# Row sums of 64 MB on one core: the scaling of the last results moved to GpSimd, and the last store cut in two halves of 64 partitions on two queues

## Chip, cores, metric

One core of one Trainium2 chip. The time is the device's, in microseconds, median of several executions. Every execution quoted was in the fast state, at a granted clock of 1.0, or, where there was a single look (e14, e15, e17), at a clock of 1.0 and of unknown state.

Words used below: the issue of a DMA is the instruction that starts it, its landing the last of the semaphore increments that report it done. The DRAIN of an engine stands in its closing part, ahead of its report to the barrier; the closing barriers are where all engines wait for each other at the end of the program. DVE is VectorE, ACT is ScalarE, POOL is GpSimd, SP is SyncE. A line such as `L193` is a line of that kernel's program; the same statement has other line numbers in other kernels. "Columns" are fp32 values of one partition.

## The reference

```python
x: float32 [32, 512, 1024]
def reference(x, divisor):                 # divisor = 1024.0
    return (np.sum(x, axis=-1) / divisor).astype(np.float32)
```

16,384 rows of 1024 values, so 128 per partition. 112 per partition go through large tiles (result `res`, stored early), the last 16 through ever smaller ones (result `fin`).

## The kernel before

The parts that matter, with cuts marked. `landed` is a semaphore of its own for the last store: the program's closing barriers run while that store is under way, and SyncE waits for it last.

```python
def close_while_storing(nc, landed):
    ...                                    # cut: finds the last store, takes it out of the body
    end.instructions = [
        with_sync(drain, on_wait=tuple(needs.values())),      # SyncE: wait for all other work
        with_sync(store, on_wait=(done,), on_update=(add,)),  # the store waits for VectorE alone
        *end.instructions[1:-1],                              # the barriers of all engines
        with_sync(last, on_update=(sub,)),                    # wait for landed >= 16
    ]
...
    res = one.tile([P, M], F32, name="res")
    fin = one.tile([P, L], F32, name="fin")
    q = one.tile([P, L], F32, name="q")
    r = one.tile([P, L], F32, name="r")    # L = 16
    nc.gpsimd.memset(r, 0.0)
...                                        # cut: loads and sums of all rows but the last two
    c = 768
    row = one.tile([P, D], F32, name="row")
    load(row, x_last[:, j, :])
    act_sum(r[:, j : j + 1], row[:, c:], by=scale)
    nc.vector.reduce_sum(out=q[:, j : j + 1], in_=row[:, :c], axis=AX)

    a, b = 448, 704                        # the very last row comes in three pieces
    pa = one.tile([P, a], F32, name="pa")
    pb = one.tile([P, b - a], F32, name="pb")
    pc = one.tile([P, D - b + 2], F32, name="pc")
    load(pa, x_last[:, L - 1, :a])
    load(pb, x_last[:, L - 1, a:b])
    load(pc[:, : D - b], x_last[:, L - 1, b:])
    nc.gpsimd.tensor_scalar_mul(out=res, in0=res, scalar1=scale)
    tc.keep_in_program_order(nc.sync.dma_start(out=o_main, in_=res))

    act_sum(pc[:, D - b : D - b + 1], pa)
    nc.vector.reduce_sum(out=pc[:, D - b + 1 :], in_=pb, axis=AX)
    nc.vector.scalar_tensor_tensor(
        out=fin[:, : L - 1], in0=q[:, : L - 1], scalar=scale, in1=r[:, : L - 1], op0=MULT, op1=ADD
    )
    scaled = one.tile([P, D - b + 2], F32, name="scaled")
    nc.vector.tensor_scalar(
        out=scaled, in0=pc, scalar1=scale, scalar2=0.0, op0=MULT, op1=ADD, accum_out=fin[:, L - 1 :]
    )
    tc.keep_in_program_order(nc.sync.dma_start(out=o_last, in_=fin))
```

## Time and profile before

| | before |
|---|---|
| time, median of the first 3 runs | 161.4 us (161.34 to 161.51) |
| span of the profile | 159.8 us |
| DMA queue, share of the span | 98.0% |
| last VectorE result | 158.28 us |
| issue of the last store, its landing | 158.31 us, 159.73 us |

The span is the time from the first to the last instruction in the profile; the time of that execution was 161.31 us, so 1.55 us lie outside the span. The DMA queue is full nearly all the way, so the change was aimed at the last 2 to 3 us, behind the last bytes. The lines of the profile stand in the prediction.

### The profile page before, as it was taken

The page shows a single profiled execution, that of the slowest core. Times are in us where ns is not written, and L with a number is a line of the kernel's source. Part 1 is how long each engine was busy: PE and PEld are TensorE (multiplying, and loading weights), DVE is VectorE, ACT ScalarE, POOL GpSimd, SP SyncE. Part 2 cuts the span into 40 slices and gives each one's busy share as a digit, 9 for nine tenths or more (in the row PEclk, how much of TensorE's full clock was granted, in tenths as well). Part 3 has the DMA queues.
Part 4 walks back from the last instruction along what each step waited for, and adds up shares of the span by engine and source line. Part 5 has one row for each costly group of instructions (what it writes and reads, how often), then busy time and mean ns, then how long its engine had stood idle before and what let it go on. Part 6 is the DMA issues. An engine that isn't in the chain of part 4 may idle for free.

```text
span 159.8 us, 139 instructions
## 1 busy us (share of the span) xinstructions
DVE 121.1 (76%) x17; ACT 19.6 (12%) x37; POOL 0.8 (0%) x6
## 2 busy tenths in 40 slices
DVE  0500059995999599978999599959995996494985
ACT  3000000000000000000000000000001900480973
POOL 0000000000000000000000000000000000001000
DMA  7999999978999999978999999978999999899993
GB/s 250 472 459 459 459 459 459 459 330 359 459 459 459 459 459 459 459 316 373 459 459 459 459 459 459 416 345 388 459 459 427 394 480 505 353 435 390 408 400 132
DMA packets 2592, 67.18 MB, mean 420 GB/s; under 512 B 544, under 2 KB 928, under 8 KB 1056
## 3 DMA queue, kind: packets, MB, share of 16 engines
q1 hardware_dynamic: 2592, 67.18, 98.0%
HBM read 67.11 MB, written 0.07 MB: 420 GB/s over the span
## 4 chain that ended last, share of the span: by engine, by line
DMA 76%; DVE 22%; SPq 1%; issue 0%; DVEq 0%
DMA t<-in_x_dram 56%; DMA row<-in_x_dram 21%; DVE res L153 20%; SPq L142 1%; DVE q L176 1%; DVE scaled L198 0%; DVE pc L193 0%; DVE fin L194 0%; DVEq L198 0%; DVEq L232 0%
## 5 line engine op out<-in xcount | busy, mean ns | idle before, releaser
L153 DVE TENSOR_REDUCE res<-t 128x14 f32<-128x14336 f32 (+3 forms) x9 | 111.2, 12360 | 34.3 <-DMA t<-in_x_dram 34.3
L147 ACT ACTIVATE junk<-t 128x1024 f32<-128x1024 f32 x16 | 16.2, 1013 | 135.9 <-DMA t<-in_x_dram 135.9
L153 DVE TENSOR_REDUCE q<-t 128x4 f32<-128x4096 f32 (+2 forms) x3 | 7.9, 2642 | 2.7 <-DMA t<-in_x_dram 2.5
L147 ACT ACTIVATION_READ_ACCUMULATOR junk<-t 128x1 f32 x16 | 3.0, 187 | 0.0
L147 ACT ACT_TABLE_LOAD x1 | 1.3, 1283 | 1.7 <-PEq L218 1.7
L189 POOL TENSOR_SCALAR res<-res 128x112 f32<-128x112 f32 x1 | 0.5, 494 | 143.8 <-DVE res L153 143.8
L176 DVE TENSOR_REDUCE q<-row 128x1 f32<-128x768 f32 x1 | 1.0, 953 | 0.0
L198 DVE TENSOR_SCALAR_CACHE_REDUCE scaled<-pc 128x322 f32<-128x322 f32 x1 | 0.5, 490 | 0.1
L147 ACT ACTIVATE junk<-pa 128x448 f32<-128x448 f32 x1 | 0.5, 548 | 0.0
L193 DVE TENSOR_REDUCE pc<-pb 128x1 f32<-128x256 f32 x1 | 0.4, 414 | 0.0
L147 ACT ACTIVATE junk<-row 128x256 f32<-128x256 f32 x1 | 0.4, 388 | 0.1
L194 DVE SCALAR_TENSOR_TENSOR fin<-q,r 128x15 f32<-128x15 f32 x1 | 0.2, 176 | 0.0
L147 ACT ACTIVATION_READ_ACCUMULATOR junk<-pa 128x1 f32 x1 | 0.2, 186 | 0.0
L147 ACT ACTIVATION_READ_ACCUMULATOR junk<-row 128x1 f32 x1 | 0.2, 185 | 0.0
L139 POOL MEMSET r<- 128x16 f32 x1 | 0.1, 112 | 1.3 <-POOLq L218 1.3
L218 POOL MEMSET const-bfloat16-1.0<- 128x1 bf16 x1 | 0.1, 103 | 0.0
L218 POOL MEMSET const-uint8-127<- 128x1 uint8 x1 | 0.1, 102 | 0.0
L218 POOL MEMSET const-float32-0.0<- 128x1 f32 x1 | 0.1, 99 | 0.2 <-issue 0.2
L218 POOL MEMSET const-float32-1.0<- 128x1 f32 x1 | 0.1, 99 | 0.0
L198 DVE DVE_READ_ACCUMULATOR scaled<-pc 128x1 f32 x1 | 0.1, 83 | 0.0
## 6 DMA issues: line engine op xcount, KB each, us to landing
t<-in_x_dram SPq DMA_DIRECT2D x7, 7168.0 KB, 35.7
t<-in_x_dram SPq DMA_DIRECT2D x1, 6144.0 KB, 33.3
t<-in_x_dram SPq DMA_DIRECT2D x1, 4096.0 KB, 26.1
t<-in_x_dram SPq DMA_DIRECT2D x2, 1024.0 KB, 18.6
t<-in_x_dram SPq DMA_DIRECT2D x1, 2048.0 KB, 30.5
row<-in_x_dram SPq DMA_DIRECT2D x1, 512.0 KB, 33.2
pa<-in_x_dram SPq DMA_DIRECT2D x1, 224.0 KB, 33.3
pc<-in_x_dram SPq DMA_DIRECT2D x1, 160.0 KB, 33.1
```

What stands on the lines that cost most here:

```text
L139: nc.gpsimd.memset(r, 0.0)
L142: tc.keep_in_program_order(nc.sync.dma_start(out=dst, in_=src))
L147: nc.scalar.activation(junk[:, :n], src, COPY, scale=by, accum_out=dst)
L153: nc.vector.reduce_sum(out=dst[:, :d], in_=t[:, :d, :], axis=AX)
L176: nc.vector.reduce_sum(out=q[:, j : j + 1], in_=row[:, :c], axis=AX)
L189: nc.gpsimd.tensor_scalar_mul(out=res, in0=res, scalar1=scale)
L193: nc.vector.reduce_sum(out=pc[:, D - b + 1 :], in_=pb, axis=AX)
L194: nc.vector.scalar_tensor_tensor(out=fin[:, : L - 1], in0=q[:, : L - 1], scalar=scale, in1=r[:, : L - 1], op0=MULT, op1=ADD)
L198: nc.vector.tensor_scalar(out=scaled, in0=pc, scalar1=scale, scalar2=0.0, op0=MULT, op1=ADD, accum_out=fin[:, L - 1 :])
L218: nc = _bacc.Bacc("TRN2", target_bir_lowering=False, num_devices=1)
```

## The change

The intent: free VectorE, which runs its last four operations nearly back to back, of one of them (the scaling of 15 columns goes to GpSimd) and of 64 columns of another (768 becomes 704); and cut the last store in halves that go out from two queues at once, so that it would land sooner. As `r` now holds one column, it is made one column wide. Two lines that order the semaphore waits of a DMA are cut below; all kernels of the experiments that were built from the changed kernel, and e1, e2, e11 and e13, have them too.

```diff
@@ close_while_storing @@
+    for engine in (SP, ACT):
+        half = [... last DMA copy of that engine ...][-1]
+        ...
+        halves[engine] = with_sync(half, on_update=(add,))
...
-    last = nc.sync.wait_ge(landed, 16).ins
+    last = nc.sync.wait_ge(landed, 32).ins
...
-        with_sync(store, on_wait=(done,), on_update=(add,)),
+        with_sync(halves[SP], on_wait=(done,)),
@@ the kernel @@
-    r = one.tile([P, L], F32, name="r")
-    nc.gpsimd.memset(r, 0.0)
+    r = one.tile([P, 1], F32, name="r")
...
-    c = 768
+    c = 704
...
-    act_sum(r[:, j : j + 1], row[:, c:], by=scale)
+    act_sum(r, row[:, c:], by=scale)
...
-    nc.vector.scalar_tensor_tensor(
-        out=fin[:, : L - 1], in0=q[:, : L - 1], scalar=scale, in1=r[:, : L - 1], op0=MULT, op1=ADD
+    nc.gpsimd.tensor_scalar_mul(out=fin[:, :j], in0=q[:, :j], scalar1=scale)
+    nc.gpsimd.tensor_scalar(
+        out=fin[:, j : j + 1], in0=q[:, j : j + 1], scalar1=scale, scalar2=r, op0=MULT, op1=ADD
     )
...
-    tc.keep_in_program_order(nc.sync.dma_start(out=o_last, in_=fin))
+    H = P // 2
+    tc.keep_in_program_order(nc.sync.dma_start(out=o_last[:H], in_=fin[:H]))
+    nc.scalar.dma_start(out=o_last[H:], in_=fin[H:])
```

More of the change, by code (lines that the diff above doesn't have):

```diff
@@ L15 @@
 SP = mybir.EngineType.SP
+ACT = mybir.EngineType.Activation
 def start_loads_at_once(nc):
@@ L53, in rank @@
     def rank(i, w):
+        if type(i).__name__ == "InstDMACopy":
+            return 1 if w.ant_name.startswith("DVE_") else 2
         own = {"DVE": "DVE_", "Activation": "Activation_", "SP": "DVE_", "Pool": "DVE_"}
@@ L71, in close_while_storing @@
     body, end = nc.main_func.blocks[1], nc.main_func.blocks[-1]
-    store = [i for i in body.instructions if i.engine == SP and type(i).__name__ == "InstDMACopy"][-1]
-    (lane,) = store.sync_info.on_update
     drain = end.instructions[0]
@@ L76, in close_while_storing @@
     needs = {w.id: w for w in drain.sync_info.on_wait}
-    assert needs[lane.id].wait_value > lane.update_value
-    needs[lane.id] = dataclasses.replace(
-        needs[lane.id], wait_value=needs[lane.id].wait_value - lane.update_value
-    )
-    (done,) = [w for w in store.sync_info.on_wait if w.ant_name.startswith("DVE_")]
+    own = dict(sync_type="semaphore", id=landed.num, ant_name=landed.name)
+    add = mybir.SyncUpdate(update_mode="sem-add-imm", update_value=16, **own)
+    sub = mybir.SyncUpdate(update_mode="sem-sub-imm", update_value=32, **own)
+    halves = {}
+    for engine in (SP, ACT):
+        half = [i for i in body.instructions if i.engine == engine and type(i).__name__ == "InstDMACopy"][-1]
+        (lane,) = half.sync_info.on_update
+        assert needs[lane.id].wait_value >= lane.update_value
+        needs[lane.id] = dataclasses.replace(
+            needs[lane.id], wait_value=needs[lane.id].wait_value - lane.update_value
+        )
+        halves[engine] = with_sync(half, on_update=(add,))
+    (done,) = [w for w in halves[SP].sync_info.on_wait if w.ant_name.startswith("DVE_")]
     assert needs[done.id].wait_value == done.wait_value
     del needs[done.id]
-    own = dict(sync_type="semaphore", id=landed.num, ant_name=landed.name)
-    add = mybir.SyncUpdate(update_mode="sem-add-imm", update_value=16, **own)
-    sub = mybir.SyncUpdate(update_mode="sem-sub-imm", update_value=16, **own)
-    last = nc.sync.wait_ge(landed, 16).ins
+    last = nc.sync.wait_ge(landed, 32).ins
     assert nc.main_func.blocks[-1].instructions[-1].name == last.name
-    body.instructions = [i for i in body.instructions if i.name != store.name]
+    body.instructions = [
+        halves[ACT] if i.name == halves[ACT].name else i
+        for i in body.instructions
+        if i.name != halves[SP].name
+    ]
     end.instructions = [
-        with_sync(drain, on_wait=tuple(needs.values())),
-        with_sync(store, on_wait=(done,), on_update=(add,)),
+        with_sync(drain, on_wait=tuple(w for w in needs.values() if w.wait_value)),
+        with_sync(halves[SP], on_wait=(done,)),
         *end.instructions[1:-1],
```

## The prediction

> **What bounds the kernel now.** I read the page first (busy tenths, rates, the chain that ended last), then the chain of work and the timeline of the last 5 us, the waits of the DMA queue, and last the DMA issues.
>
> The page's second and third parts: busy tenths in 40 slices of 4 us, and the queue's share of the span.
>
> ```profile
> DVE  0500059995999599978999599959995996494985
> DMA  7999999978999999978999999978999999899993
> q1 hardware_dynamic: 2592, 67.18, 98.0%
> HBM read 67.11 MB, written 0.07 MB: 420 GB/s over the span
> ```
>
> The 16 DMA engines are taken for 98% of the span and VectorE (DVE) for 76%: 67 MB of input at 420 GB/s set the time. The change touches no load, so about 157 of the 161 us are out of its reach. What is left is the tail, behind the last bytes. The timeline from 155 us on (start, duration):
>
> ```profile
> 156.18 0.39 ACT L147 ACTIVATE junk<-row 128x256 f32<-128x256 f32 x1
> 156.18 0.95 DVE L176 TENSOR_REDUCE q<-row 128x1 f32<-128x768 f32 x1
> 156.50 0.18 ACT L147 ACTIVATION_READ_ACCUMULATOR junk<-row 128x1 f32 x1
> 156.72 0.55 ACT L147 ACTIVATE junk<-pa 128x448 f32<-128x448 f32 x1
> 157.17 0.18 DVE L194 SCALAR_TENSOR_TENSOR fin<-q,r 128x15 f32<-128x15 f32 x1
> 157.20 0.19 ACT L147 ACTIVATION_READ_ACCUMULATOR junk<-pa 128x1 f32 x1
> 157.26 0.41 DVE L193 TENSOR_REDUCE pc<-pb 128x1 f32<-128x256 f32 x1
> 157.79 0.49 DVE L198 TENSOR_SCALAR_CACHE_REDUCE scaled<-pc 128x322 f32<-128x322 f32 x1
> 158.20 0.08 DVE L198 DVE_READ_ACCUMULATOR scaled<-pc 128x1 f32 x1
> 158.31 0.34 SPq L201 DMA_DIRECT2D out_dram<-fin  x1
> ```
>
> See that DVE runs four instructions without a pause from 156.18 to 158.28 us, and that ScalarE (ACT) is done at 157.39. The store starts 0.03 us after DVE. The DMA issues (last column: us from issue to landing), with the waits of the DMA queue:
>
> ```profile
> pc<-in_x_dram SPq DMA_DIRECT2D x1, 160.0 KB, 33.1
> pb<-in_x_dram SPq DMA_DIRECT2D x1, 128.0 KB, 33.1
> out_dram<-res SPq DMA_DIRECT2D x1, 56.0 KB, 11.5
> out_dram<-fin SPq DMA_DIRECT2D x1, 8.0 KB, 1.4
> ```
>
> ```profile
> SPq L232 <- DMA out_dram<-res: 0.6, 1, 0.6
> SPq L201 <- DVE scaled L198: 0.5, 1, 0.5
> ```
>
> Added to their issue times in the trace (123.87, 124.39, 146.17, 158.31), the records put the landings at 157.02 (pb), 157.50 (pc), 157.71 (the big store of res) and 159.73 us (the last store). The span ends at 159.76. So from 156.18 on DVE is the bound: pc has been there for 0.29 us when the last operation starts at 157.79, and SyncE has been free since 157.78 for a store that starts at 158.31. After that comes one store of 8 KB that takes 1.42 us. Its parts by the trace's records: 0.34 us issue, 0.50 us until the first packet (159.15), 0.21 us of packets (to 159.36), then the 16 semaphore increments arrive from 159.56 to 159.73, most 8 ns apart. The barriers that close the program run beside it and end at about 159.50, so they have 0.25 us to spare.
>
> **What the Trainium skill says.** "DMA: Bandwidth & Descriptors", Rules for kernel authors, has this very case: two transfers to disjoint partition halves are not worth it, for both spread over the same 16 engines; one transfer of 128 partitions is advised. Its section Issuing engines are not separate DMA queues says that issuing from several engines only saves sequencer time. The trace has only one queue so far and can't show it[...]. "Perfetto Trace Analysis", DMA Instruction — HWDGE, says that the descriptor generator is shared between sequencers and locked while one uses it; no run here shows it yet. "GPSIMD Engine Reference", 3.1, gives a GpSimd instruction two software dispatch hops; [...]494 ns for 112 columns, while a memset of 16 columns takes 112 ns.
>
> **The change part by part.**
>
> 1. The row is split 704/320 instead of 768/256. DVE reductions to one column take 1220 ns (1024 elements), 953 (768) and 414 (256), so (953-414)/512 = 1.05 ns an element: 704 elements take 886 ns, 67 ns less. ACT: (548-388)/192 = 0.83 ns an element, so 320 take 441 ns, 53 ns more. ACT's next operation waits for pa (landed 156.70, start 156.72); with the longer row ACT is ready at about 156.66. So ACT's end stays at 157.39.
>
> 2. The 15-column scaling leaves DVE. It cost 157.26-157.13 = 0.12 us between the row reduction's end and the pb reduction's start (the latter overlaps its tail). Now the row ends at 156.18+0.89 = 157.07, and pb may follow at once: pb landed at 157.02, and DVE started 0.02 us after a landing in the case of row. So pb starts at 157.04 to 157.08, ends at 157.46 to 157.50.
>
> 3. The last operation started 0.12 us after the pb reduction's end (157.79-157.67). So it starts at 157.57 to 157.62. Other floors: pc's landing 157.50+0.02; ACT's 157.39. Both hold less than 0.1 us before it, so about a further 0.05 us of speed-up would have been lost. It is 0.49 us long, so the store can be issued at 158.10 to 158.14: gain 0.17 to 0.22 us, taken as 0.20.
>
> 4. GpSimd does the scaling instead. The 14 columns need the next-to-last row's results (156.16): start 156.2, an estimate of 0.3 us from the 494 ns. The single column needs the row reduction (157.07) and takes an estimated 0.3 to 0.4 us: done by about 157.5. That is 0.5 us before DVE's last operation ends at about 158.07. So both lie beside other work, at a cost of 0. The memset of r falls away at 1.7 us, where nothing waits for it.
>
> 5. The store in halves. Each engine still gets eight 64-byte descriptors, and two completion descriptors instead of one, so the packets save nothing. 32 increments must reach one semaphore; if they come 8 ns apart as in before, that is 0.13 us more than 16. If the issue of a half is shorter than 0.34 us, some is won back: the input loads of 1 to 7 MB have issues of 0.33 to 0.47 us, as long as the 8 KB store's, so the issue hardly goes by size and I expect at most 0.05 us. If the generator is shared, the half that comes second is late by some part of 0.34 us. I take +0.10 us as the middle, from -0.05 to +0.40.
>
> Sum: -0.20 + 0.10 = -0.10 us, 161.4 to 161.3 us, with the span going from 159.8 to 159.7.
>
> **Rivals.** A: the halves run truly side by side, each with shorter issue and packets, and the store shortens by 0.1 us or more: 161.4-0.2-0.1 = 161.1. For it: most of the 1.42 us is latency, and two latencies can overlap. Against it: they overlap with nothing that was serial before, as the size of the store was hardly in the 1.42. B: the halves serialize, or ACT's first and only DMA issue is slow to start: +0.35 on the store eats the 0.20 gained, 161.55. For it: the skill's locked generator. Also, the closing barriers wait for ACT's issue too; with 0.25 us to spare they would bind only if ACT's issue took over 0.6 us. C: the gain on DVE is lost because GpSimd becomes the last producer: the two stores and the closing drain wait for it. It would need the one-column operation to take over 0.9 us, against 0.49 for 112 columns; then 161.4 or more. D: a second DMA queue costs something outside the span (time minus span is now 161.3-159.8 = 1.5 us, of which the profile shows nothing): by its nature not to be sized here.
>
> **Range and chances.** The three runs before spread 0.17 us by themselves, and loads may land differently by as much from run to run. Parts 1 to 3 are sure to about 0.05 us, part 5 is the loose one, from -0.05 to +0.40; so 160.95 to 161.65, and 161.25 as the single number, a little under the sum, as the change was made by someone who presumably kept it for a reason. 2% is 3.2 us. Nothing in the tail is that long but the whole stretch from the last landing to the end, 159.76-157.50 = 2.3 us. So faster by 2% is out of reach, and slower by 2% needs an unknown cost of the second queue: 0.005 and 0.01.
>
> **What would show it.** In the changed kernel's timeline the row reduction must be about 886 ns, no DVE instruction must stand between it and the pb reduction, and the last operation must start 0.17 to 0.22 us earlier against pc's landing. GpSimd's two operations must end before 158.0. The two stores must show issue to landing of 1.35 to 1.8 us, the later one ending the span. I am wrong if the last operation waits for pc instead of pb, if GpSimd ends after DVE, if ACT's issue starts more than 0.2 us after SyncE's, or if the time moves with an unchanged span.

## The result

| | before | changed |
|---|---|---|
| time, median of 6 runs | 161.31 us | 162.07 us (162.01 to 162.15) |
| span of the profile | 159.8 us | 160.3 us |
| last VectorE result | 158.28 us | 158.30 us |
| landing of the last store | 159.73 us | 160.30 us |

The ratio is 1.0045, 95% interval 1.0032 to 1.0058. (A ratio here is the mean time of one kernel's fast runs over that of the other's of the same rounds, so not quite the ratio of the medians.) The change is clearly 0.76 us slower, where 0.06 to 0.15 us faster had been predicted with a range that ended at 161.65.

The timeline of the changed kernel (start, duration in us, engine, line, operation):

```profile
156.28 0.89 DVE L186 TENSOR_REDUCE q<-row 128x1 f32<-128x704 f32 x1
156.29 0.26 POOL L204 TENSOR_SCALAR fin<-q 128x14 f32<-128x14 f32 x1 [10.22 <-DVE q L163]
...
157.26 0.42 DVE L203 TENSOR_REDUCE pc<-pb 128x1 f32<-128x256 f32 x1
157.27 0.26 POOL L205 TENSOR_SCALAR fin<-q,r 128x1 f32<-128x1 f32 x1 [0.72 <-DVE q L186]
...
157.80 0.49 DVE L209 TENSOR_SCALAR_CACHE_REDUCE scaled<-pc 128x322 f32<-128x322 f32 x1
158.22 0.08 DVE L209 DVE_READ_ACCUMULATOR scaled<-pc 128x1 f32 x1
158.33 0.53 SPq L213 DMA_DIRECT2D out_dram<-fin  x1
158.33 0.54 ACTq L214 DMA_DIRECT2D out_dram<-fin  x1
```

The 15-column scaling is gone from DVE, GpSimd's two are out of the way by 157.54, the row reduction is 64 columns shorter, and yet the pb reduction starts at 157.26 as before and the last operation at 157.80 instead of 157.79. Something else gave the gain back. Then both issues take 0.53 and 0.54 us, where the single one took 0.34.

The DMA issues of the changed kernel (last column: us from issue to landing):

```profile
pc<-in_x_dram SPq DMA_DIRECT2D x1, 160.0 KB, 33.3
pb<-in_x_dram SPq DMA_DIRECT2D x1, 128.0 KB, 33.4
...
out_dram<-fin SPq DMA_DIRECT2D x1, 4.0 KB, 1.7
out_dram<-fin ACTq DMA_DIRECT2D x1, 4.0 KB, 2.0
```

pb and pc are issued as before but take longer to land (33.1 both before): by the records 0.24 and 0.18 us longer, so that they land at 157.24 and 157.65 instead of 157.02 and 157.50. That is why DVE gained nothing: it now waits for pb. The chain of work that ended last (start, duration in us) has the load of pb ahead of the pb reduction, where it had DVE's own operations before:

```profile
123.85 33.39 DMA pb<-in_x_dram
157.24 0.02 issue
157.26 0.43 DVE pc L203
```

And half a store lands later than a whole one did (1.4).

The instructions of the closing part, of all engines, first before and then in the changed kernel (duration in ns: shortest/median/longest; first and last start in us):

```profile
L232 SPq DRAIN  x3: 7/7/133, 157.8 to 159.1; - x3
...
L232 PEldq EVENT_SEMAPHORE  x2: 51/51/51, 159.0 to 159.5; - x2
```

```profile
L245 SPq DRAIN  x3: 7/7/363, 157.9 to 159.8; - x3
...
L245 ACTq DRAIN  x2: 8/320/632, 158.9 to 159.8; - x2
...
L245 PEldq EVENT_SEMAPHORE  x2: 51/51/51, 159.7 to 160.2; - x2
```

The drain that follows the store's issue, and stands ahead of the barrier, took 0.13 us; now SyncE's takes 0.36 and ScalarE's 0.63 (ScalarE's 0.70 before was spent early, from 156.7 us on). The last barrier instruction starts at 159.5 before and at 160.2 now.

So there were three things to explain: the late loads, the slow halves, and 0.15 us more outside the span (162.03-160.34 = 1.69 us against 1.55). My theories:

- **Loads.** `r` shrank from 64 to 4 bytes (32 with padding), so every tile allocated after it (the last tiles, `row`, `pa`, `pb`, `pc`) moved by 32 bytes. In the records, a packet of 1280 bytes (the rows of pc) takes 60.9 ns on average, 55.0 before. Rivals: chance, or GpSimd's work at the same time.
- **Store.** Two issues at the same moment stretch each other. Rivals: a half is slow in itself; ScalarE's queue is slow; it happens only together with the other parts.

### The profile page after: what moved, and what is told of

Read it like the earlier page. It is cut to its first block, busy times and chain, and to the rows that moved or that the text cites. A ratio compares the mean times of both kernels' runs of the same rounds, so it can differ in the third digit from the quotient of the medians.

```text
span 160.3 us, 142 instructions
## 1 busy us (share of the span) xinstructions
DVE 121.0 (75%) x16; ACT 19.7 (12%) x37; POOL 1.2 (1%) x7
## 4 chain that ended last, share of the span: by engine, by line
DMA 76%; DVE 21%; SPq 1%; issue 0%; DVEq 0%
DMA t<-in_x_dram 55%; DMA pb<-in_x_dram 21%; DVE res L163 20%; SPq L152 1%; DVE scaled L209 0%; DVE pc L203 0%; DVEq L209 0%; DVEq L245 0%
## 5 line engine op out<-in xcount | busy, mean ns | idle before, releaser
L186 DVE TENSOR_REDUCE q<-row 128x1 f32<-128x704 f32 x1 | 0.9, 886 | 0.1
## 6 DMA issues: line engine op xcount, KB each, us to landing
row<-in_x_dram SPq DMA_DIRECT2D x1, 512.0 KB, 33.4
```

## The experiments

e14, e15 and e17 were run for one look, all others 4 to 6 times; each "before" is of the same chip and session, and several experiments share one. One table first, since single loads come late by chance (`row` by 0.66 us in e7) and blur the times. It follows one execution, the profiled one, piece by piece, from the records of the trace: from the landing of `row` to the last DVE result, and from there to the end of the last barrier instruction (of TensorE), to the landing of the last store, and to the end of the execution as timed.

```text
run                        row lands   last DVE result to
                           to last     barriers'  last store  end of
                           DVE result  end        landed      the time    (us)
before                       2.127      1.239      1.445       3.026
changed                      2.041      1.944      2.002       3.730
e1  one store                2.033      1.239      1.437       3.031
e2  one store, aligned       1.923      1.244      1.438       3.030
e11 the same again           1.914      1.245      1.442       3.034
e3  halves only              2.124      1.945      2.003       3.725
e6  32-byte shift only       2.118      1.240      1.438       3.022
e7  changed, aligned         1.941      1.947      1.996       3.739
e4  halves, one queue        2.127      2.301      2.365       4.084
e5  one store, from ACT      2.117      1.291      1.481       3.080
e8  halves "apart"           2.117      2.713      2.775       4.502
e9  64 partitions alone      2.128      1.661      1.727       3.449
e17 64 part. x 8 col. alone  2.127      1.657      1.716       3.445
e14 32 partitions alone      2.128      1.250      1.378       3.032
e15 112 partitions alone     2.126      1.253      1.442       3.040
e16 split 32 + 96            2.126      1.308      1.547       3.099
e10 two x 8 columns          2.120      1.296      1.600       3.085
e10b the same, apart         2.128      1.239      1.436       3.027
e12 late barrier (failed)    2.126      1.938      2.137       3.720
e13 arrive first             1.912      0.900      1.577       2.948
```

### e1: the changed kernel with one store again

```diff
-    H = P // 2
-    tc.keep_in_program_order(nc.sync.dma_start(out=o_last[:H], in_=fin[:H]))
-    nc.scalar.dma_start(out=o_last[H:], in_=fin[H:])
+    tc.keep_in_program_order(nc.sync.dma_start(out=o_last, in_=fin))
     # and close_while_storing as before
```

> The changed kernel with one store of 128 partitions from SyncE again; scaling on GpSimd, the 704/320 split and the one-column r stay. Theory (the halves cost the time, the late loads eat the gain on VectorE): landing of the last store back to 1.42 us after its issue, time back at 161.25 to 161.4 us, that is no better than before, since pb still lands near 157.2. Rival (the scaling on GpSimd is what costs): stays at 161.7 or more.

161.41 us against 161.39 (ratio 1.0001, 0.9989 to 1.0014). Issue 0.344 us, landing 1.41. So the halves cost all of the difference, and the rest of the change, as it stands, is worth nothing: pb took 33.4 us again.

### e2 and e11: e1 with r wide again

```diff
-    r = one.tile([P, 1], F32, name="r")
+    r = one.tile([P, 16], F32, name="r")[:, :1]
```

> As e1, but r is 16 columns wide again (one used), so that the tiles of the last loads lie at multiples of 64 bytes as before. Theory (the 32-byte shift slows the last loads): 1280-byte packets back to 55 ns, pb lands at 157.0, pc at 157.5, the last VectorE operation starts at 157.57 and the time is 161.05 to 161.15, about 0.2 us under e1 and under before. Rival (late landings were chance or come from GpSimd's scaling): same as e1 within 0.08 us.

161.18 us, beside 161.41 for e1 in the same rounds: 0.23 us for a declaration. The 1280-byte packets were back at 55.0 ns, and `row` to pb took 0.863 us as before (0.862; e1: 0.977). In the profiled execution `row` itself landed 0.19 us later than before, so that pb still landed at 157.21. To see whether that was chance, and whether the lead is clear of noise, it was run again:

> The kernel of e2 once more (scaling on GpSimd, one store, tiles at multiples of 64 bytes), to see whether its lead over before is clear of noise, and for a trace without a slow load packet: time 161.1 to 161.25 us, ratio 0.9985; pb lands near 157.0 and the last VectorE operation starts at 157.57.

160.95 us against 161.41 in a noisier session (ratio 0.9969, 0.9953 to 0.9984; e2 had 0.9988, 0.9976 to 1.0001). The timeline of e11:

```profile
156.06 0.89 DVE L178 TENSOR_REDUCE q<-row 128x1 f32<-128x704 f32 x1
...
156.93 0.42 DVE L195 TENSOR_REDUCE pc<-pb 128x1 f32<-128x256 f32 x1
...
157.46 0.49 DVE L201 TENSOR_SCALAR_CACHE_REDUCE scaled<-pc 128x322 f32<-128x322 f32 x1
...
157.98 0.34 SPq L204 DMA_DIRECT2D out_dram<-fin  x1
```

Now the pb reduction follows at the row reduction's heels (156.06+0.89 = 156.95), and from the landing of `row` to the last result DVE takes 1.914 us instead of 2.127. That is the gain of 0.21 us that the prediction had worked out as 0.17 to 0.22. (Its times in us are lower than predicted, since all of this execution's loads came earlier.)

### e6: the shift alone

```diff
     r = one.tile([P, L], F32, name="r")
+    one.tile([P, 8], F32, name="gap")
     nc.gpsimd.memset(r, 0.0)
```

> The kernel before with an unused 32-byte tile after r, which moves the tiles of the last loads to addresses that are 32 modulo 64, and nothing else. Theory of the shift: 1280-byte packets 60 ns instead of 55, pb lands about 0.2 us and pc about 0.15 us later; as VectorE has 0.29 us to spare against pc but almost none against row (+0.1), the time rises by 0.1 to 0.2 us. Rival (chance): packets 55 ns, time within 0.05 us of before.

161.48 us against 161.39 (ratio 1.0005, 0.9993 to 1.0018), so by time alone unclear, just under the 0.1 to 0.2 us that the theory expected. The trace decides: packets of 1280 bytes took 59.9 ns, and `row` to pb took 0.985 us (0.862 before). The DMA issues of e6:

```profile
pc<-in_x_dram SPq DMA_DIRECT2D x1, 160.0 KB, 33.3
pb<-in_x_dram SPq DMA_DIRECT2D x1, 128.0 KB, 33.4
```

They are the changed kernel's numbers, in a kernel without any of its other parts. In the kernel before, DVE reaches pb late anyway (chain of 2.118 us against 2.127), so only the later landing of `row` is felt; in e1, freed of an operation, DVE waits, and loses 2.033-1.918 = 0.115 us in the chain (1.918 is the mean of e2 and e11). The three traces with moved tiles (changed, e1, e6) have 0.977 to 0.985 us from `row` to pb, the 17 others 0.857 to 0.926. What leads from the packets to that delay stays open: pa's and pb's packets grew by 1.2 and 0.6 ns on average, which at 8 packets each per engine is only about 15 ns. GpSimd's work is cleared by e2, e7 and e11, which have it and have fast packets.

The Trainium skill, "DMA: Bandwidth & Descriptors", How a descriptor splits into AXI transactions, says that transactions start at multiples of 256 bytes and that a piece that doesn't start there costs additional beats. The page's account is of what is read; here it is the written side, in SBUF, that moved. The addresses that the allocator gives when these kernels are built fit in direction: `row`, `pa`, `pb` and `pc` lie at multiples of 256 before, at 224 modulo 256 in the changed kernel and at 32 in e6. My expectations spoke of 64 bytes; these runs don't tell 64 from 256. The size of the cost does not follow the page: by its count, an estimate, 1280 bytes take 40 beats at a multiple of 256, 41 at 32 and 47 at 224, but the packets took 55.0, 59.9 and 60.9 ns, nearly the same at both. And it is uneven: 74.0 to 75.2 ns for 1792 bytes, 46.0 to 46.6 for 1024.

### e3 and e7: the halves alone, and the changed kernel with the loads mended

e3 is the kernel before with the store's edit of the diff (and the order of DMA waits that comes with it); e7 is the changed kernel with r 16 columns wide as in e2.

> The kernel before with nothing but the store in two halves. Theory (descriptor generation is serial, two issues at once stretch each other): each issue about 0.53 us, landings 1.7 and 2.0 us, span +0.55, time 161.3+0.6 to 161.3+0.8, so 161.9 to 162.1. Rival (the halves are late only together with GpSimd or with the later loads): under +0.3 us.

> The changed kernel with nothing but r made 16 columns wide, so that the last tiles lie at multiples of 64 bytes. If the two costs are independent: 162.07-0.23 = 161.8 us, with 1280-byte packets at 55 ns and both stores landing 1.7 and 2.0 us after issue. Rival (the late landing comes from the end of the program being later for another reason): stays at 162.0.

e3: 161.99 us against 161.39 (1.0037, 1.0023 to 1.0051); issues 0.53 and 0.55, landings 1.70 and 1.97. e7: 161.83 us against 161.4 (1.0033, 1.0019 to 1.0047). Both as expected: the halves cost 0.70 us behind the last DVE result whether or not the rest of the change is there, and the two costs add up.

### e5: the whole store from ScalarE

```diff
-    tc.keep_in_program_order(nc.sync.dma_start(out=o_last, in_=fin))
+    nc.scalar.dma_start(out=o_last, in_=fin)     # and waited for as before
```

> The kernel before with its last store whole, from ScalarE alone. Theory (issues that overlap stretch each other, ScalarE's queue is not slow in itself): issue 0.33 to 0.40 us, landing 1.40 to 1.50 us, span within 0.1 us of before; time minus span 1.69 us if a second queue costs 0.14 us outside the span, 1.55 if not. Rival (a first and only issue on ScalarE is slow): issue 0.5 us or more, landing 1.7 us or more.

161.44 us against 161.4 (1.0003, 0.9989 to 1.0016). Issue 0.373, landing 1.449: ScalarE's queue is not slow, though this was its first and only issue; from the last DVE result to the end it is 3.080 us against 3.026, so it costs 0.05 us. And the time minus the span was 1.57 us: the second queue costs nothing outside the span.

### e4: both halves from SyncE

```diff
-    nc.scalar.dma_start(out=o_last[H:], in_=fin[H:])
+    tc.keep_in_program_order(nc.sync.dma_start(out=o_last[H:], in_=fin[H:]))
```

> The kernel before with the store in two halves of 64 partitions, both issued by SyncE, one after the other. Theory (the work before a store's first packet is done for one store at a time, whatever queue it comes from): second issue starts 0.35 to 0.4 us after the first, lands 1.4 us after its own issue, so 1.75 to 1.85 us after the first; span +0.35 to +0.45, less than the +0.53 of two queues. Time minus span stays at 1.55 us if the additional 0.14 us outside the span belong to the second queue. Rival (two halves cost the same from any queue): span +0.55. Rival (it is the second queue alone): no more than +0.1.

162.46 us against 161.4 (1.0064, 1.005 to 1.0078): worse than my theory allowed. Its two issues:

```profile
158.48 0.53 SPq L212 DMA_DIRECT2D out_dram<-fin  x1
159.06 0.58 SPq L213 DMA_DIRECT2D out_dram<-fin  x1
```

Nothing else was being issued beside the first half, and it still took 0.530 us to issue and landed at 1.706. So my theory of two issues that stretch each other falls. The time minus the span was 1.69 us, with only one queue in use.

### e8: a failed attempt to hold the halves apart

ScalarE's half goes through three small copies on ScalarE first, so as to be issued later.

```diff
+    late = fin
+    for k in range(3):
+        copy_of = one.tile([P, L], F32, name=f"late{k}")
+        nc.scalar.activation(copy_of[H:], late[H:], COPY)
+        late = copy_of
-    nc.scalar.dma_start(out=o_last[H:], in_=fin[H:])
+    nc.scalar.dma_start(out=o_last[H:], in_=late[H:])
```

> The kernel before with the store in two halves from two queues, but ScalarE's half is issued about 0.6 us later, after three small copies of its data on ScalarE. Theory (only issues that overlap stretch each other): each issue back at 0.33 to 0.40 us, each lands about 1.40 us after its own issue, the span +0.6 to +0.75 by the delay alone. Rival (a half, or a second queue, costs more by itself): issues stay at 0.53 us and landings at 1.7 us or more after their issue.

162.85 us against 161.4 (1.0089). It did not hold them apart: SyncE waits for all other work ahead of its store, ScalarE's copies included, so its half went out 0.10 us after ScalarE's. One thing it shows: this time SyncE's half came second, and landed last (1.91 us after its issue, ScalarE's at 1.75). In e3 ScalarE's half came second and landed last. So as far as these two traces show, it goes by the order and not by the engine.

### e9: half a store alone

```diff
-    tc.keep_in_program_order(nc.sync.dma_start(out=o_last, in_=fin))
+    tc.keep_in_program_order(nc.sync.dma_start(out=o_last[: P // 2], in_=fin[: P // 2]))
```

The result is wrong, here and in e14, e15 and e17.

> The kernel before with a last store of partitions 0 to 63 alone, from SyncE; the other half is never stored, so the result is wrong on purpose. Theory (a store of 64 partitions is slower than one of 128 by its shape): issue 0.53 us, landing 1.70 us, span +0.29, time +0.4 if the 0.14 us outside the span come with it. Rival (only two stores at a time are slow): issue 0.34 us or less, landing 1.42 us or less.

Issue 0.530 us and landing 1.70, with nothing beside it; 161.69 us against 161.41 in a noisy session (1.0013, 0.9995 to 1.003), but 3.449 us from the last DVE result to the end against 3.026. A store of 64 partitions is slower than one of 128 in itself.

### e14, e15, e17: is it the size?

32 partitions, 112 partitions, and 64 partitions of 8 columns: the same edit with other bounds, one look each.

> The kernel before with a last store of partitions 0 to 31 alone, wrong on purpose. If stores of fewer than 128 partitions are all issued the slow way: issue 0.5 us or more, landing 1.65 to 1.75 us, for a quarter of the bytes. If the issue goes by the number of partitions: 0.5 us would fall well below that.

> The kernel before with a last store of partitions 0 to 111 alone, wrong on purpose. If only all 128 partitions are issued the fast way: issue 0.5 us or more, landing 1.65 to 1.8 us, although it has almost the bytes of the whole store. Rival (something particular to 64): 0.34 us and 1.42 us.

> The kernel before with a last store of 64 partitions and only 8 columns (2 KB), wrong on purpose. If the count of 64 partitions is what is slow: issue 0.53 us, landing about 1.7 us. If it is the 4 KB, or 64 pieces of 64 bytes: issue about 0.35 us, landing about 1.4 us.

The last issue of the timelines of e9, e14, e15 and e17, in this order:

```profile
158.75 0.53 SPq L201 DMA_DIRECT2D out_dram<-fin  x1
```

```profile
158.16 0.36 SPq L201 DMA_DIRECT2D out_dram<-fin  x1
```

```profile
158.28 0.36 SPq L201 DMA_DIRECT2D out_dram<-fin  x1
```

```profile
158.38 0.53 SPq L201 DMA_DIRECT2D out_dram<-fin  x1
```

64 partitions are slow with 4 KB and with 2 KB; 32 partitions with the same 2 KB, and 112 with 7 KB, are fast. So it is neither the bytes nor "fewer than 128", but something about the count of 64. What it is, these runs don't say. e14 shows one thing more: its store landed 0.067 us sooner after the last result than before's (1.378 against 1.445), and the end did not come sooner (3.032 against 3.026).

### e16: another split

```diff
-    H = P // 2
+    H = P // 4        # in e3: 32 partitions from SyncE, 96 from ScalarE
```

> The kernel before with its last store split 32 (SyncE) and 96 (ScalarE) partitions instead of 64 and 64. Theory (64 partitions are slow in themselves, splitting is nearly free): issues of 0.34 to 0.39 us each, closing barriers 1.25 to 1.30 us after the issue, from issue to end 3.04 to 3.09 us against 3.00, time 0.05 us over before. Rival (the halves cost because there are two): from issue to end 3.3 us or more.

161.55 us against 161.34 (1.0008, 0.9994 to 1.0021; later loads in some executions), 3.099 us from the last DVE result to the end against 3.026. Its two stores:

```profile
158.52 0.36 SPq L213 DMA_DIRECT2D out_dram<-fin  x1
158.52 0.39 ACTq L214 DMA_DIRECT2D out_dram<-fin  x1
```

Landings 1.35 and 1.52. The split into 32 and 96 costs 0.07 us where 64 and 64 cost 0.70; and 0.05 of the 0.07 is what a store from ScalarE costs alone (e5).

### e10 and e10b: halves by columns

Each half has 8 columns of all 128 partitions. In e10 both wait for the last DVE result; in e10b ScalarE's columns, ready earlier, go out 0.94 us earlier.

```diff
-    H = P // 2
-    tc.keep_in_program_order(nc.sync.dma_start(out=o_last[:H], in_=fin[:H]))
-    nc.scalar.dma_start(out=o_last[H:], in_=fin[H:])
+    H = L // 2
+    tc.keep_in_program_order(nc.sync.dma_start(out=o_last[:, H:], in_=fin[:, H:]))
+    nc.scalar.dma_start(out=o_last[:, :H], in_=fin[:, :H])
```

> The kernel before with its last store in two halves of 8 columns, each of all 128 partitions, from SyncE and ScalarE at the same moment. Theory (the shape of 64 partitions is slow, and two stores at once queue up by some 0.27 us): issues 0.34 to 0.37 us, the first lands at 1.42 us, the second 0.2 to 0.3 us later, span +0.2 to +0.3. Rival (any two stores at once stretch each other): issues of 0.5 us and landings of 1.7 and 2.0 us, span +0.55.

> As e10, but ScalarE's half holds the columns that are ready first and goes out about 0.9 us before SyncE's. Theory: no overlap, so SyncE's half has its issue of 0.34 us and lands at 1.42 us; span as before within 0.05 us, and time minus span shows whether a second store or queue costs anything outside the span (1.55 us if not). Rival (two queues in use cost by themselves): +0.2 us or more.

e10: 161.7 us against 161.41 (1.0007, 0.9986 to 1.0027), in the noisy session. Its stores, by its DMA issues:

```profile
out_dram<-fin SPq DMA_DIRECT2D x1, 4.0 KB, 1.4
out_dram<-fin ACTq DMA_DIRECT2D x1, 4.0 KB, 1.6
```

Issues 0.343 and 0.378 us, as each engine has alone (before 0.344, e5 0.373): at this shape the two issues don't hold each other up, and only the second landing is later, by 0.16 us. The barriers end as in e5, which has ScalarE's store alone (1.296 and 1.291). It shows something else. Against before, its store landed 0.155 us later after the last result, its barriers ended 0.057 us later, and the time was 0.059 us longer. **The time went with the barriers, not with the landing.** e16 agrees (landing 0.10 us later, barriers 0.069, end 0.073), and so does e14. e10b: 161.29 us (0.9992, 0.9975 to 1.0009), every interval as before.

With this in mind, look down the table. In all traces but e13's, the time ends 1.780 to 1.792 us after the barriers, while time minus span, which ends with the wait for the landing, runs from 1.45 (e10) to 1.71 (e7). The "0.15 us outside the span" (0.14 in the expectations) is no cost of its own: it is the distance from the barriers to the landing, which shrank where the drains grew.

### e12: an attempt to delay the barriers alone

```diff
     act_sum(pc[:, D - b : D - b + 1], pa)
+    for n in (D, 576):
+        junk = psum.tile([P, D], F32, name="junk")
+        nc.scalar.activation(junk[:, :n], row[:, :n], COPY)
```

> The kernel before, with two additional operations on ScalarE that nothing uses, so that it arrives at the closing barrier about 0.2 us after SyncE would; the store is untouched. Theory (the time ends 1.79 us after the closing barriers, not with the landing of the store): barriers end 0.15 to 0.25 us later, the store lands 1.42 us after its issue as before, the span is the same within 0.03 us, and the time counted from the store's issue rises from 3.00 to 3.15 to 3.25 us. Rival (the landing, at the end of the span, sets the time): from the issue to the end still 3.00 us.

161.99 us against 161.35 (1.0041), and a miss: SyncE waits for ScalarE ahead of its store too, so the store was issued at 159.08, 0.73 us after the last result, and barriers and landing moved together. It tells nothing apart. (It is e8's mistake again: I had not looked at what that drain waits for.)

### e13: arrive at the barrier, then store

On top of e2: SyncE waits for VectorE's last result, reports to the barrier, and only then issues the store.

```diff
     end.instructions = [
-        with_sync(drain, on_wait=tuple(needs.values())),
-        with_sync(store, on_wait=(done,), on_update=(add,)),
-        *end.instructions[1:-1],
+        with_sync(drain, on_wait=(done, *waits)),
+        *rest[:at],                      # up to SyncE's report to the first barrier
+        with_sync(store, on_wait=(), on_update=(add,)),
+        *rest[at:],
         with_sync(last, on_update=(sub,)),
     ]
```

> The kernel of e2 with SyncE arriving at the closing barrier (after VectorE's last result) before it issues the store instead of after it. Theory (issue and drain of the store stand before the barrier and so on the path): barriers end 0.2 to 0.35 us earlier against the last result, while the store lands 0.05 to 0.1 us later; if the barrier alone sets the time, 160.7 to 160.95 us; if the landing takes over, nearer 161.1. Rival (the landing sets the time already): 0.05 to 0.1 us slower than e2.

161.03 us against 161.35 (ratio 0.9981, 0.9968 to 0.9993). The barriers end 0.900 us after the last result instead of 1.244, so 0.34 us earlier; the store is issued 0.14 us later (158.25 us, with the result at 158.08), and lands that much later. From the last result to the end it is 2.948 us against 3.030: 0.08 us of the 0.34 arrive. Here the time ends 2.05 us after the barriers and 1.34 us after the span, less than in any other run. So where barriers and landing were moved apart by an edit, the end followed neither of them alone. That fits a rule of two branches: the end comes 1.79 us after the barriers or 1.34 us after the wait for the landing, whichever is later, so that a second bound takes over. The rule is inferred, and its second figure rests on this one kernel.

e13 and e11 beat the kernel before by 0.2 and 0.3%, far below 2%; e2's 0.1% alone is not clear of noise.

## Why the prediction was wrong, point by point

1. **The row reduction** (886 ns, ACT's end unmoved): right. 886 ns measured. ACT's end did move, by 0.17 us, but with the late landing of pa.
2. and 3. **The operation that leaves DVE, gain 0.17 to 0.22 us**: right as mechanism and size, where the loads land as before: 0.204 us (e2) and 0.213 us (e11) between the landing of `row` and the last result. In the changed kernel it was 0.086, and a `row` that landed 0.10 us later took that too. The step that failed is the premise "the change touches no load". It touched the addresses that loads write to: r's narrowing moved the last tiles by 32 bytes, which e1, e2 and e6 show. In part 3, the prediction says that both other floors lie less than 0.1 us ahead of the last operation; this holds for pc (0.05 to 0.10), not for ACT's 157.39 (0.18 to 0.23). It changes nothing here. The allocation could have been printed beforehand, and the skill's section on transactions had been at hand.
4. **GpSimd's two operations beside other work**: right; 0.26 us each, done 0.75 us ahead of the last result, so rival C did not occur. The two figures that the prediction set beside the two dispatch hops (494 ns and 112 ns) show no hop; that 14 columns and one column take 261 and 264 ns does show a time that hardly goes by size.
5. **The store, "+0.10 us as the middle, from -0.05 to +0.40"**: wrong. This is the step that took the time out of the range (with the late loads alone, e1 has 161.41 us). From the last result to the end it costs 3.730-3.026 = 0.704 us. Two terms failed:
   - "the issue hardly goes by size and I expect at most 0.05 us" gain: true by bytes (of the figures behind it, the 0.47 us are those of pb, 128 KB; the loads of 1 to 7 MB took 0.33 to 0.43), but a store of 64 partitions takes 0.53 us to issue and a longer drain (0.36 against 0.13 us), alone 3.449-3.026 = 0.42 us to the end (e9). No row of the profile before had such a store. The remaining 0.28 us of the 0.70 come with the second half: they are the difference between e3 and e9. That it queues behind the first is a reading, not shown. Two stores of other shapes cost 0.06 to 0.07 us (e10, e16), of which ScalarE's store alone makes 0.05 (e5), so nearly nothing is left there for queueing.
   - The bound itself. The prediction added the landing to the time and gave the barriers "0.25 us to spare". By the constant distance of 1.78 to 1.79 us, the time followed the barriers in the kernel before too; the landing is what had something to spare (by the rule above, 161.31-159.76-1.34 = 0.21 us). With one store the two move together, which hides it. A store that only lands sooner, with no shorter issue or drain, would have saved nothing, as e14's one look has it. Rival A counted on that and on a shorter issue, and the issue of a half is longer.

   Rival B (the halves serialize, +0.35) was nearest. Its remark that barriers would bind "only if ACT's issue took over 0.6 us" was wrong for the reason just given. Rival D (a second queue costs something outside the span) looked confirmed by 1.69 us against 1.55, and is refuted by e5 and e4.

The sum of the profiled executions: -0.21 us from DVE's own work, +0.22 us from loads (0.10 for `row`, 0.12 for pb in the chain; how much of the 0.10 is chance in this one execution stays open, timed runs give the shift 0.23 us between e1 and e2), +0.70 us from the halves: +0.71, and 162.03-161.31 = +0.72 was measured.

Open: why 64 partitions are slow to issue, what makes the second of two such stores 0.27 us later, how slower packets delay pb by 0.12 us, and whether the alignment that matters is 64 or 256 bytes. That the barriers set the time rests on the distances in 19 traces, not on a run that moved them alone.

## What to carry to other kernels

Changing the width of a small tile moves every tile allocated after it; where the tail depends on small loads, compare the allocated addresses of both kernels. Before you shorten the last transfer, find out which event ends the time: compare over several runs what keeps a constant distance to it (here the closing barriers, ahead of which stand the issue of the store and its drain). And measure a split transfer alone, half by half: a half can be dearer than the whole.

## What the Trainium skill lacked or had wrong

- "DMA: Bandwidth & Descriptors", Rules for kernel authors, advises against two transfers to disjoint partition halves, and is right in that: +0.70 us. Its reason, that the two serialize because both share the same engines, does not account for it: two overlapping stores of other shapes cost 0.06 to 0.07 us (e10, e16), 0.05 of that by ScalarE's issuing one of them (e5), and half a store alone costs 0.42 (e9). No page has it that 64 partitions take 0.53 us to issue, against 0.34 to 0.39 for 32, 96, 112 and 128.
- The same page, Latency and other measured facts, gives about 600 ns to the first byte on this path, without saying from when it counts. Here the first packet came 0.84 us after the start of the issue for 128 partitions and 1.17 us for the first half of 64, or 0.50 and 0.64 us after the end of the issue.
- "Perfetto Trace Analysis", DMA Instruction — HWDGE, puts the wait for the shared generator into the reported issue. Two simultaneous issues in e10 took 0.343 and 0.378 us, hardly more than alone (0.344, 0.373). With halves of 64 the issues took 0.53 and 0.54 us, as one alone does (0.53, e9), and what the second cost more showed behind the issues, in the drains: 0.36 and 0.63 us.
- "DMA: Bandwidth & Descriptors", How a descriptor splits into AXI transactions, agrees in direction for loads into SBUF (55.0 to 60.9 ns for 1280 bytes off a multiple of 256), but gives no durations, and its count of beats does not give the sizes: 41 beats at 32 modulo 256 took 59.9 ns, 47 at 224 took 60.9.
- "Runtime: NRT & Kernel Launch", The ~15µs preamble/postamble breakdown, lists what the runtime adds behind a kernel, but neither it nor another page says which event of the kernel the device's time follows. Here it ended 1.78 to 1.79 us after the closing barriers in 19 of 20 traces, and 2.05 us in the one in which the store was issued behind SyncE's report to the barrier (e13).
